# A gated-mixer layer on one core: half of the convolution's input tiles by seven products in place of eight, and 20 host tiles for 36 attention units

## The chip, the cores and the metric

The kernel runs on one core of a Trainium2 chip. The metric is the device time of one execution in microseconds (us); the median of the runs shown is used. Engines are named as in the profile: PE (TensorE's matmuls), PEld (its weight loads), DVE (VectorE), ACT (ScalarE), POOL (GpSimd), SP (SyncE, which issues most DMAs).

## The reference

One layer of a streaming encoder for 1024 prompt frames and 32 sample frames, width 1024, in float32:

```python
h = rms_norm(x, g_mix)
z = h @ w_in                       # [q | k | v | conv_h | conv_B | conv_C | gate_a | gate_b]
a = window_attn(q, k, v) @ w_attn_out          # 16 heads, 4 kv heads, band of 2 to 3 chunks of 64
u = cc * ch
conv = u[t-2] * conv_w[0] + u[t-1] * conv_w[1] + u[t] * conv_w[2]
bo = (cb * conv) @ w_conv_out
x = x + (sigmoid(ga) * a + sigmoid(gb) * bo) @ w_mix_out
x = x + memory_cross_attention(rms_norm(x)) ; x = x + relu(rms_norm(x) @ w_up)**2 @ w_down
```

The last two rows of `u` of each request group are an output too (`o_conv`).

## The kernel before

**Arithmetic.** Each float32 operand is split into a rounded part and a rest, and a product is three matmuls. Tokens lie in three chunks c of 384, 384 and 288 columns. A weight tile is 1024 rows by 128 columns, held as 128x1024; `gemm` (L195) runs it over one chunk in 24 matmuls. `fetch_w` (L147) loads a tile by SP, `issue_w` (L164) splits it on ACT (L129) and DVE (L130), two tiles ahead of use, in the order of the list `worder`.

**Stages** in the order of the program, one weight tile after another:

1. Norms, the first query tiles and the memory's keys and values, to about 85 us.
2. The attention stage, to about 547 us. 32 *hosts*, each one weight tile over three chunks: the 24 convolution tiles C, H and B of the eight f, six query tiles, one key tile and one gate tile. 36 attention units (4 kv heads times 8 blocks and a sample block) are strung between the hosts' chunks, each as `scores`, `turn` (transposes) and `values`: about one unit per host. Between scores and turn lies a softmax on DVE, ACT and POOL. `do_conv` (L633) puts the scaling of t for C and B on POOL (L649, L664, L666) and stores B's result to `bc_d`.
3. A gate tile, three `gate_a2` and eight `do_attn_out` (L831), to about 657 us. In these the operands of the seven-product form are made (`gx_steps`).
4. Seven `gate_pair` (L936): the tiles of gate_a and gate_b of one f, over chunks 0 and 1, by seven half products (`product`, L887, 12 matmuls) in place of eight, in the Strassen-Winograd form: each needs two sums of the pair's weights (`g_sum`) and sums of the activations (b11, b21, t2, n1, n3, b22, n4). Chunk 2 goes by `gate_c2`, an ordinary gemm. To about 775 us.
5. `do_conv_out` (L1072), for each chunk eight tiles: bc times w_conv_out, times the gate, plus the attention's part `m1_d`, added on POOL for f = 0 to 6 (L1081) and on DVE for f = 7. Then `do_mix` (L1087), which needs all eight results of its chunk. Then cross-attention and the MLP, whose matrices also go partly by weight sums.

**Weight sums on POOL.** `sum_step` (L729) makes them in *pieces*: a load by POOL's own DMA queue (L739 or L741) into one of two tiles (`ws` and `xacc`, by turns), four adds of 128x256 (L746), a store to HBM (L750 or L752). A piece of kind "g" is half a gate pair's sum of w_in, "u" one of w_up, and the other 32 are of w_down. One call starts the load of the next piece and finishes the piece before it. The pieces are a list, 14 g, then 32 of w_down, then 4 u; `sum_step` is called at 29 places in the hosts, then in stages 3 and 4. All its instructions are pinned, that is they keep their order on POOL. A tile's next load waits until its store has landed.

**What sets the order.** The program is written as a list of items; a scheduler with a model of the machine then fixes the order of the instructions on each engine, except of those that are pinned. Each engine runs its list strictly in order, so POOL's other operations wait behind a piece that waits.

Of the kernel before, what the change touches and what calls it, by code (L numbers as in the profile page):

```python
# [40 lines left out]
def hybrid_step(ctx: ExitStack, tc: tile.TileContext, io):  # L41
# [492 lines left out]
    def do_KS(kv):  # L534
# [18 lines left out]
        ksp[kv] = (hi, lo, ch, cl, b, bs)

    class Unit:
# [5 lines left out]
        def scores(self):  # L561
            kv, p = self.kv, self.p
            hi, lo, ch, cl, bias, bs = ksp[kv]
            if self.sample:
                G, nk = 1, 256
# [34 lines left out]
            for h in range(G):  # L600
                dve.tensor_scalar_mul(stl[:, h, :nk], stl[:, h, :nk], rec[:, h : h + 1])
# [31 lines left out]
    def do_conv(which, f, extras=()):  # L633
        def fn(w):
# [84 lines left out]
    pieces = [("g", f, q) for f in PAIRS for q in range(2)]  # L719
# [9 lines left out]
    def sum_step():  # L729
        old = W.pop("new", None)  # L730
        if pieces:
            at = pieces.pop(0)
            t = sum_tile(len(pieces))
            if at[0] in ("g", "u"):
                kind, f, q = at
                for e in range(2):
                    src = io["w_in"][34 + 8 * e + f] if kind == "g" else io["w_up"][UP[f][e]]
# [5 lines left out]
        if old:  # L743
# [3 lines left out]
            if at[0] in ("g", "u"):  # L747
                kind, f, q = at
                for w in range(2):
                    pin(pool_e.dma_start((gsum_d[f - 1] if kind == "g" else usum_d[f])[:, w, :, 256 * q : 256 * q + 256], t[:, 2 * w : 2 * w + 2]))  # L750
# [184 lines left out]

    def gate_pair(f):  # L936
        def take(key):
            k, w = ready.pop(0)
            assert k == key, (k, key)
            return w  # L940
# [26 lines left out]
        if f == 1:  # L967
            pump(4)
# [1092 lines left out]
```

## Time and profile before

| | us |
|---|---|
| median of 3 runs | 1737.74 (1737.34 to 1739.08) |
| profiled execution, device time | 1739.95 |
| its span | 1738.2 |
| TensorE busy | 1722.8 |
| POOL busy | 600.7 |
| last attention store issued on POOL | 549.50 |
| last weight-sum store issued on POOL | 773.73 |
| end of the first mix tile, on DVE | 839.43 |

A timeline row gives start, duration, engine, line, operation, output<-input, and in brackets the idle time before it and what ended it. A row of a group gives the number of instructions, their busy time and mean, and after the bar the engine's idle time ahead of them with its releasers. A row of windows gives a stretch, its length, the busy time of PE, PEld, DVE, ACT and POOL, the granted clock, the DMA engines' busy share and the rate in GB/s.

### The profile page before, as it was taken

Reading aid. Unit: us, or ns where it says so; the run is one execution under the profiler, and the core shown is the slowest. Engines: PE = TensorE matmul, PEld = TensorE weight load, DVE = VectorE, ACT = ScalarE, POOL = GpSimd, SP = SyncE. Lnnn points to the kernel's source line nnn. Section 1 sums busy time; section 2 is a strip of 40 time slices with the busy share of each in tenths; the row PEclk is TensorE's granted clock in tenths of the full one; section 3 lists DMA queues with packets and bytes.
Section 4 is the critical chain, followed back from the end, with each engine's and each line's share of the span. In section 5 each row is a group of like instructions: output and inputs, shape, how many; then the busy total and the mean of one; then the engine's idle time right before and its main releaser. Section 6 shows DMA issues by size and latency. Waiting matters only on the chain.

```text
span 1738.2 us, 32563 instructions
## 1 busy us (share of the span) xinstructions
PE 1722.8 (99%) x12238; PEld 1707.1 (98%) x12238; DVE 1194.9 (69%) x2276; ACT 854.0 (49%) x1666; POOL 600.7 (35%) x671
## 2 busy tenths in 40 slices
PE   9999999999999999999999999999999999999998
PEld 8999999999999999999999999999999999999998
DVE  7776776867766656555677888687666686546675
ACT  8653533535335324434556666765444553333444
POOL 0026366453643444552225242106555410000122
PEclk9999999999999999999999999999999999999999
DMA  5343344333445888867766667676666695554555
GB/s 186 98 131 121 125 134 137 131 131 133 150 141 193 291 302 282 294 221 233 272 222 200 216 229 253 226 266 201 221 220 220 215 316 186 187 196 164 199 165 168
DMA packets 179853, 346.60 MB, mean 199 GB/s; under 512 B 18656, under 2 KB 101248, under 8 KB 179568
## 3 DMA queue, kind: packets, MB, share of 16 engines
q1 hardware_dynamic: 163504, 290.07, 50.5%
q0 software_dynamic: 15568, 53.68, 8.9%
q8 instruction: 96, 1.57, 0.4%
q10 hardware_dynamic: 624, 0.77, 0.1%
q14 instruction: 61, 0.50, 0.1%
HBM read 250.73 MB, written 93.14 MB: 198 GB/s over the span
## 4 chain that ended last, share of the span: by engine, by line
PE 93%; DMA 3%; DVE 2%; ACT 1%; issue 1%; POOL 0%; SPq 0%; DVEq 0%; ACTq 0%; POOLq 0%
PE acc L200 13%; PE acc L202 13%; PE acc L201 13%; PE acc L892 6%; PE acc L893 6%; PE acc L894 6%; PE acc L1832 6%; PE acc L1834 6%; PE acc L1833 6%; PE pc L892 2%; PE pc L894 2%; PE pc L893 2%; PE pt L609 2%; PE sc L584 1%; PE sc L583 1%; PE pa L201 1%
## 5 line engine op out<-in xcount | busy, mean ns | idle before, releaser
L129 ACT CAST wh<-wr 128x1024 fp32r<-128x1024 f32 (+1 forms) x214 | 223.8, 1046 | 361.9 <-PE acc L1833 124.8
L130 DVE TENSOR_TENSOR wl<-wr,wh 128x1024 fp32r<-128x1024 f32 (+1 forms) x214 | 276.6, 1293 | 109.7 <-ACT wh L129 108.4
L200 PE MATMUL acc<-X,wh 128*128 128x384 f32 (+1 forms) x864 | 281.4, 326 | 0.0
L201 PE MATMUL acc<-X,wh 128*128 128x384 f32 (+1 forms) x864 | 278.9, 323 | 0.0
L202 PE MATMUL acc<-X,wl 128*128 128x384 f32 (+1 forms) x864 | 277.8, 322 | 0.0
L287 POOL TENSOR_TENSOR xacc<-xacc,ct 128x384 f32<-128x384 f32 (+1 forms) x55 | 74.8, 1364 | 364.0 <-ACT ct L285 362.3
L201 PEld LDWEIGHTS acc<-X,wh 128*128 128x128 f32 x864 | 162.7, 188 | 1.6 <-DVE X L291 0.7
L200 PEld LDWEIGHTS acc<-X,wh 128*128 128x128 f32 x864 | 162.4, 188 | 0.8
L202 PEld LDWEIGHTS acc<-X,wl 128*128 128x128 f32 x864 | 162.4, 188 | 0.1
L200 PE MATMUL acc<-Y,wh 128*128 128x384 f32 (+1 forms) x432 | 139.8, 324 | 2.2 <-DVE ct L1080 2.2
L202 PE MATMUL acc<-Y,wl 128*128 128x384 f32 (+1 forms) x432 | 139.3, 323 | 1.3 <-DMA wl<-wl_d 1.3
L201 PE MATMUL acc<-Y,wh 128*128 128x384 f32 (+1 forms) x432 | 139.5, 323 | 0.0
L129 ACT CAST PTh<-pt 128x512 fp32r<-128x512 f32 (+3 forms) x94 | 45.9, 517 | 112.2 <-PE pt L609 110.5
L1834 PE MATMUL acc<-n,wl 128*128 128x264 f32 x352 | 100.0, 285 | 0.8 <-DVE wl L130 0.8
L1832 PE MATMUL acc<-n,wh 128*128 128x264 f32 x352 | 100.3, 285 | 0.2 <-ACT wh L129 0.2
L1833 PE MATMUL acc<-n,wh 128*128 128x264 f32 x352 | 100.1, 284 | 0.0
L746 POOL TENSOR_TENSOR ws<-ws 128x256 f32<-128x256 f32 x100 | 96.2, 962 | 5.8 <-DMA ws<-in_w_up 0.2
L746 POOL TENSOR_TENSOR xacc<-xacc 128x256 f32<-128x256 f32 x100 | 85.4, 854 | 5.7 <-DMA xacc<-in_w_in 0.4
L200 PEld LDWEIGHTS acc<-Y,wh 128*128 128x128 f32 x432 | 81.1, 188 | 3.1 <-DVE ct L1080 3.1
L202 PEld LDWEIGHTS acc<-Y,wl 128*128 128x128 f32 x432 | 81.1, 188 | 1.6 <-DMA wl<-wl_d 1.6
L201 PEld LDWEIGHTS acc<-Y,wh 128*128 128x128 f32 x432 | 81.1, 188 | 0.5 <-DVE Y L803 0.5
L595 ACT ACTIVATE S<-S,nmx 128x257 f32<-128x257 f32 (+1 forms) x132 | 64.2, 488 | 19.9 <-DVE nmx L590 18.6
(446 smaller groups left out, 5562.2 us busy)
## 6 DMA issues: line engine op xcount, KB each, us to landing
wr<-in_w_up SPq DMA_DIRECT2D x53, 512.0 KB, 4.4
wr<-in_w_in SPq DMA_DIRECT2D x52, 512.0 KB, 3.6
wr<-wsum_d SPq DMA_DIRECT2D x40, 512.0 KB, 3.5
wr<-in_w_conv_out SPq DMA_DIRECT2D x24, 512.0 KB, 4.0
wr<-in_w_mix SPq DMA_DIRECT2D x24, 512.0 KB, 4.5
wr<-in_w_down SPq DMA_DIRECT2D x24, 512.0 KB, 3.6
n_d<-Z SPq DMA_DIRECT2D x32, 264.0 KB, 4.3
xacc<-in_w_down POOLq DMA_DIRECT2D x16, 512.0 KB, 4.8
```

The costliest lines, as they stand in the source:

```text
L129: act.copy(hi, src)
L130: dve.tensor_sub(lo, src, hi.bitcast(F32))
L200: pe.matmul(out, wh[:, a], hi, start=(k == 0), stop=False)
L201: pe.matmul(out, wh[:, a], lo, start=False, stop=False)
L202: pe.matmul(out, wl[:, a], hi, start=False, stop=(k == len(acts) - 1))
L746: pin(pool_e.tensor_tensor(t[:, to], t[:, x], t[:, y], op=ALU.add))
L892: pe.matmul(acc, wh[:, a], hi, start=(start and k == 0), stop=False, skip_group_check=True)
L893: pe.matmul(acc, wh[:, a], lo, start=False, stop=False, skip_group_check=True)
L894: pe.matmul(acc, wl[:, a], hi, start=False, stop=(k == 3), skip_group_check=True)
L1832: pe.matmul(a, wh[:, s], hi, start=(t == 0 and k == 0), stop=False, skip_group_check=True)
L1833: pe.matmul(a, wh[:, s], lo, start=False, stop=False, skip_group_check=True)
L1834: pe.matmul(a, wl[:, s], hi, start=False, stop=(t == 1 and k == 7), skip_group_check=True)
```

## The change

Four things are changed together.

- **Twelve convolution tiles go by seven products.** The C, H and B tiles of f = 4 to 7 leave the hosts and become six `conv_pair` (C, H, B of f = 4 and 5, then of 6 and 7), each in the form of a gate pair, ahead of the seven gate pairs. Their sums add 12 pieces of kind "g", at the front of the list; `gsum_d` grows from 7 to 13 pairs.
- **20 hosts for 36 units.** A table `begin` gives the third of a host (a chunk) in which each unit's scores begin, its turn comes two thirds later and its values three. `sum_step` is called in 18 hosts.
- Half of the heads' scaling by the reciprocal goes from DVE to ACT (`act.mul`), and the loads of the cached keys come in a step of their own (`do_KC`).
- In the gate pairs u2 and v lie in tiles that exist anyway (`tmp`, `g22`); the third weight tile of the pairs (`third`) and the loads of the operands (`pump(4)`) begin at the first conv pair; `o_conv` is stored in two halves.

```diff
+    HBC = {"H": 0, "B": 1, "C": 2}
+    CPAIRS = [(which, f) for f in (4, 6) for which in "CHB"]
+    ptiles = [(10 + 8 * HBC[which] + f, 11 + 8 * HBC[which] + f) for which, f in CPAIRS]
+    ptiles += [(34 + f, 42 + f) for f in PAIRS]
-    pieces = [("g", f, q) for f in PAIRS for q in range(2)]
+    pieces = [("g", i, q) for i in range(len(ptiles)) for q in range(2)]
     pieces += [(j, t, i) for j in range(4) for t in range(2) for i in range(4)]
     pieces += [("u", i, q) for i in range(2) for q in range(2)]
...
-                dve.tensor_scalar_mul(stl[:, h, :nk], stl[:, h, :nk], rec[:, h : h + 1])
+                if h < G // 2:
+                    act.mul(stl[:, h, :nk], stl[:, h, :nk], rec[:, h : h + 1])
+                else:
+                    dve.tensor_scalar_mul(stl[:, h, :nk], stl[:, h, :nk], rec[:, h : h + 1])
...
-    conv = [(which, f) for f in range(NF) for which in "CHB"]
+    conv = [(which, f) for f in range(4) for which in "CHB"]
-    hosts += take(6) + [("Q", 1, 0), ("Q", 1, 1)]
-    hosts += [("K", 1)] + take(5) + [("Q", 2, 0), ("Q", 2, 1)]
-    hosts += take(6) + [("Q", 3, 0), ("Q", 3, 1)]
-    hosts += take(7) + [("G", 0)]
+    hosts += take(3) + [("Q", 1, 0), ("Q", 1, 1)]
+    hosts += [("K", 1)] + take(2) + [("Q", 2, 0), ("Q", 2, 1)]
+    hosts += take(3) + [("Q", 3, 0), ("Q", 3, 1)]
+    hosts += take(4) + [("G", 0)]
+    begin = [[1, 2, 3, 5, 6, 8, 10, 11, 13]] + [[0, 1, 3, 5, 6, 8, 10, 11, 13]] * 2 + [[0, 1, 3, 4, 6, 7, 9, 10, 12]]
...
+            slots[at][3].append(u.scores)
+            slots[at + 2][1].append(u.turn)
+            slots[at + 3][0].append(u.values)
...
-        if i % 2 and i > 1 or i > 3:
+        if i > 1:
             extras.append((1, sum_step))
...
+    def conv_C(f, c, x, s):
+        n = CH[c][1]
+        t = ct2[f, c] = slot(ga_pool, f"Ga{c}", n, F32)
+        if c == 2:
+            dve.tensor_mul(t, x, R[2])
+            pool_e.tensor_tensor(t, t, R[2], op=ALU.mult)
+        elif s is None:
+            act.copy(t, x)
+        else:
+            dve.tensor_sub(t, x, s)
+    def conv_H(f, c, x, s):
...
+            pool_e.tensor_copy(u[:, 258:260], prm[:, STATE0 + 2 * f : STATE0 + 2 * f + 2])
...
+        u = cu[f, c] = slot(G["pool"], f"Gb{c}", n, F32)
+        if s is None:
+            dve.tensor_mul(u, x, t)
+        else:
+            dve.tensor_sub(u, x, s)
+            pool_e.tensor_tensor(u, u, t, op=ALU.mult)
+    def conv_edges(f):
+        pool_e.tensor_copy(cu[f, 2][:, 0:2], cu[f, 1][:, 382:384])
...
+    def conv_B(f, c, x, s):
...
+        if c == 2:
+            act.mul(b, u[:, :m], taps[0])
...
+        else:
+            act.mul(b, u, taps[2])
...
+        if c == 2:
+            pool_e.tensor_tensor(t[:, :npr], b[:, :npr], R[c][:, :npr], op=ALU.mult)
+            pool_e.tensor_tensor(t[:, npr:], b[:, npr + 2 :], R[c][:, npr:], op=ALU.mult)
+            dve.tensor_mul(t, x, t)
+        elif s is None:
+            dve.tensor_mul(t, x, t)
+        else:
+            dve.tensor_sub(t, x, s)
+            pool_e.tensor_tensor(t, t, b, op=ALU.mult)
+        sp.dma_start(bc_d[c][:, f], t)
+    def conv_pair(i):
...
+        product(A1, w1, 0, op("b11"), True)
+        s1 = Y["top"].tile([P, 384], F32, tag="s1", name=nm("s1"))
+        act.copy(s1, A1)
...
+        product(A1, w1, 1, op("b21"), False)
+        out(f, 0, A1, None)
+        pump(0)
+        out(f, 2, gate_c2(w1), None)
...
+        product(B, w4, 0, op("t2"), True)
...
+        sum_step()
...
+        out(f + 1, 1, B, v)
+        sum_step()
...
+        if which == "H":
+            conv_edges(f)
+            conv_edges(f + 1)
...
+    for i, (t1, t2) in enumerate(ptiles):
+        worder.extend([("w_in", t1), ("g_sum", i, 0), ("g_sum", i, 1), ("w_in", t2)])
+        if i < len(CPAIRS):
+            item(lambda i=i: conv_pair(i))
+        else:
+            item(lambda f=PAIRS[i - len(CPAIRS)]: gate_pair(f))
```

In the changed program L757 are the adds of a piece, L750 and L752 its loads, L761 and L763 its stores; L962 is POOL's product in `conv_C`, L982 that in `conv_H`, L985 to L987 the copies in `conv_edges`, L998 and L1002 ACT's `act.mul` in `conv_B`, L1010, L1011 and L1017 POOL's products there, L1034 the copy of s1, L1209 POOL's add of the conv output.

POOL's order before, from the last pieces to the first adds of the conv output (usum_d and in_w_up belong to kind "u", ct to the conv output):

```order
L750 DMA usum_d<-ws_7671 128x2x256 x2
L739 DMA ws_7775<-in_w_up 128x2x256 x2
L746 TENSOR_TENSOR xacc_7728<-xacc_7728 128x256 x4
L750 DMA usum_d<-xacc_7728 128x2x256 x2
L746 TENSOR_TENSOR ws_7775<-ws_7775 128x256 x4
L750 DMA usum_d<-ws_7775 128x2x256 x2
L1081 TENSOR_TENSOR ct_9363<-ct_9363,ct_9336 128x384
L1081 TENSOR_TENSOR ct_9415<-ct_9415,ct_9388 128x384
L1081 TENSOR_TENSOR ct_9467<-ct_9467,ct_9440 128x384
```

POOL's order after, at the first adds of the conv output (wsum_d is a piece of w_down):

```order
L757 TENSOR_TENSOR xacc_8204<-xacc_8204 128x256 x4
L763 DMA wsum_d<-xacc_8204 128x1024
L1209 TENSOR_TENSOR ct_9499<-ct_9499,ct_9472 128x384
L750 DMA xacc_8354<-in_w_up 128x2x256 x2
L757 TENSOR_TENSOR ws_8248<-ws_8248 128x256 x2
L1209 TENSOR_TENSOR ct_9551<-ct_9551,ct_9524 128x384
L757 TENSOR_TENSOR ws_8248<-ws_8248 128x256 x2
L763 DMA wsum_d<-ws_8248 128x1024
L1209 TENSOR_TENSOR ct_9603<-ct_9603,ct_9576 128x384
L750 DMA ws_8400<-in_w_up 128x2x256 x2
```

Before, all pieces stood ahead of the first add; now the last piece of w_down and the u pieces stand between the first adds of chunk 0.

POOL's order after, in the first H pair (Gb and Ga are u and t of `conv_H`, u_... the third chunk's u; nothing stands here in before):

```order
L752 DMA xacc_6290<-in_w_down 128x1024
L757 TENSOR_TENSOR ws_6250<-ws_6250 128x256
L982 TENSOR_TENSOR Gb_1282_7119<-Gb_1282_7119,Ga_1254_6923 128x384
L757 TENSOR_TENSOR ws_6250<-ws_6250 128x256
L985 COPY u_7196<-Gb_1282_7119 128x2
L982 TENSOR_TENSOR Gb_1284_7141<-Gb_1284_7141,Ga_1256_6944 128x384
L757 TENSOR_TENSOR ws_6250<-ws_6250 128x256
L985 COPY u_7062<-Gb_1284_7141 128x2
L757 TENSOR_TENSOR ws_6250<-ws_6250 128x256
```

The products of u and the two-column copies into the third chunk's u stand between the adds of a w_down piece, behind its load.

ACT's order after, at the first B pair (wh is a weight tile's split, s_ the copy s1):

```order
L1002 ACTIVATE ct_7241<-Gb_1273_7035,prm 128x384
L129 CAST wh_7144<-wr_1278_7070 128x1024
L129 CAST wh_7165<-wr_7148 128x1024
L998 ACTIVATE ct_7272<-u_7062,prm 128x290
L129 CAST wh_7223<-wr_7169 128x1024
L1002 ACTIVATE ct_7334<-Gb_1282_7119,prm 128x384
L1034 COPY s_1297_7221<-acc_7206 128x384
L129 CAST wh_7281<-wr_1300_7227 128x1024
```

The reads of u_7062 and Gb_1282, which POOL writes, stand ahead of the copy of s1 and of a weight's split.

More of the change, by code (lines that the diff above doesn't have):

```diff
@@ L736, in sum_step @@
                 for e in range(2):
-                    src = io["w_in"][34 + 8 * e + f] if kind == "g" else io["w_up"][UP[f][e]]
+                    src = io["w_in"][ptiles[f][e]] if kind == "g" else io["w_up"][UP[f][e]]
                     src = src.rearrange("p (h c) -> p h c", h=2)
@@ new lines, in conv_pair @@
+    def conv_pair(i):
+        which, f = CPAIRS[i]
+        t1, t2 = ptiles[i]
+        out = {"C": conv_C, "H": conv_H, "B": conv_B}[which]
+        op = lambda kind: [gop[kind, k] for k in range(4)]
+        w1 = take_w(("w_in", t1))
+        if i == 0:
+            cvt.append(Y["top"].tile([P, 4, 4], F32, name="cvt2"))
+            third.update(n=2, pool=Y["top"])
+            fetch_w()
+            pump(4)
+        A1, B, C = (acc_tile([P, 384]) for _ in range(3))
+        product(A1, w1, 0, op("b11"), True)
+        s1 = Y["top"].tile([P, 384], F32, tag="s1", name=nm("s1"))
+        act.copy(s1, A1)
+        issue_w()
+        fetch_w()
+        product(A1, w1, 1, op("b21"), False)
+        out(f, 0, A1, None)
+        pump(0)
+        out(f, 2, gate_c2(w1), None)
+        issue_w()
+        fetch_w()
+        w4 = take_w(("g_sum", i, 0))
+        product(B, w4, 0, op("t2"), True)
+        u2 = slot(G["pool"], "Gb0", 384, F32)
+        dve.tensor_sub(u2, B, s1)
+        sum_step()
+        w3 = take_w(("g_sum", i, 1))
+        product(C, w3, 1, op("n1"), True)
+        v = slot(G["pool"], "Gb1", 384, F32)
+        dve.tensor_add(v, C, s1)
+        product(B, w3, 0, op("n3"), False)
+        out(f + 1, 1, B, v)
+        sum_step()
+        product(C, w4, 1, op("b22"), False)
+        out(f, 1, C, u2)
+        issue_w()
+        fetch_w()
+        w2 = take_w(("w_in", t2))
+        product(B, w2, 1, op("n4"), False)
+        out(f + 1, 0, B, s1)
+        issue_w()
+        fetch_w()
+        out(f + 1, 2, gate_c2(w2), None)
+        if which == "H":
+            conv_edges(f)
+            conv_edges(f + 1)
+        if which == "H" and f + 1 == NF - 1:
+            sp.dma_start(io["o_conv"][:, 4:], cvt[0])
@@ L985, in gate_pair @@
         fetch_w()
-        w4 = take(("g_sum", f - 1, 0))
+        w4 = take(("g_sum", len(CPAIRS) + f - 1, 0))
         product(B, w4, 0, op("t2"), True)
         load_a(1)
-        u2 = Y["top"].tile([P, 384], F32, tag="u2", name=nm("u2"))
-        dve.tensor_sub(u2, B, s1)
+        t = tmp(384)
+        dve.tensor_sub(t, B, s1)
         sum_step()
@@ L993, in gate_pair @@
             pump(1)
-        w3 = take(("g_sum", f - 1, 1))
+        w3 = take(("g_sum", len(CPAIRS) + f - 1, 1))
         product(C, w3, 1, op("n1"), True)
-        v = Y["top"].tile([P, 384], F32, tag="v", name=nm("v"))
-        dve.tensor_add(v, C, s1)
+        g22 = gate_slot(1, f)
+        dve.tensor_add(g22, C, s1)
         product(B, w3, 0, op("n3"), False)
-        g22 = gate_slot(1, f)
-        dve.tensor_sub(g22, B, v)
+        dve.tensor_sub(g22, B, g22)
         sg[1][f] = into(g22, g22)
```

98 lines of the change are left out of this document (58 added, 40 removed).

## The prediction

> **What bounds the kernel now.** I read the page's summary first, then the windows by stage, then the POOL timeline, because TensorE looks full and the change hands POOL more work. The page:
>
> ```profile
> span 1738.2 us, 32563 instructions
> ...
> PE 1722.8 (99%) x12238; PEld 1707.1 (98%) x12238; DVE 1194.9 (69%) x2276; ACT 854.0 (49%) x1666; POOL 600.7 (35%) x671
> ...
> PE 93%; DMA 3%; DVE 2%; ACT 1%; issue 1%; POOL 0%; SPq 0%; DVEq 0%; ACTq 0%; POOLq 0%
> ```
>
> PE holds 99% of the span and 93% of the chain that ended last; POOL is 35% busy and on no link of that chain. The windows, one row each for the attention stage, the attention output projection, the gate pairs and the start of the conv output (columns: span; busy us of PE, weight load, DVE, ACT, POOL; clock; DMA share; GB/s):
>
> ```profile
> 100.00:545.00 445.00, 445.00 (x2875) 438.15 (x2874) 317.68 (x795) 194.86 (x475) 214.54 (x316) 1.00 0.39 129
> 545.00:657.00 112.00, 111.96 (x712) 111.54 (x711) 67.06 (x97) 39.14 (x78) 52.62 (x67) 1.00 0.89 297
> 657.00:775.00 118.00, 118.00 (x731) 118.00 (x730) 74.72 (x99) 51.03 (x84) 63.88 (x75) 1.00 0.82 271
> 775.00:800.00 25.00, 25.00 (x156) 25.00 (x154) 10.58 (x16) 7.12 (x11) 1.18 (x2) 1.00 0.59 194
> ```
>
> PE waits nowhere in these 700 us, at a granted clock of 1.00, so fewer matmuls are worth their full time as long as nothing else becomes late. POOL's "busy" (52.62 of 112) misleads: it leaves out waiting and DMA issue. Its timeline in the same stretch:
>
> ```profile
> 549.50 0.70 POOL L631 DMA_DIRECT2D ao_d<-AO  x1 [4.04 <-DVE AO L628]
> ...
> 550.65 3.73 POOL L746 TENSOR_TENSOR xacc<-xacc 128x256 f32<-128x256 f32 x4
> 554.79 0.56 POOL L752 DMA_DIRECT2D wsum_d<-xacc  x1 [0.41 <-POOL xacc L746]
> 559.74 0.54 POOL L741 DMA_DIRECT2D xacc<-in_w_down  x1 [4.38 <-DMA wsum_d<-xacc]
> 560.29 5.57 POOL L746 TENSOR_TENSOR ws<-ws 128x256 f32<-128x256 f32 x4
> ...
> 632.80 0.54 POOL L741 DMA_DIRECT2D ws<-in_w_down  x1 [4.81 <-DMA wsum_d<-ws]
> 633.35 3.80 POOL L746 TENSOR_TENSOR xacc<-xacc 128x256 f32<-128x256 f32 x4
> 637.56 0.59 POOL L752 DMA_DIRECT2D wsum_d<-xacc  x1 [0.41 <-POOL xacc L746]
> 642.97 0.54 POOL L741 DMA_DIRECT2D xacc<-in_w_down  x1 [4.83 <-DMA wsum_d<-xacc]
> ...
> 727.19 4.43 POOL L746 TENSOR_TENSOR ws<-ws 128x256 f32<-128x256 f32 x4
> ...
> 737.55 4.28 POOL L746 TENSOR_TENSOR xacc<-xacc 128x256 f32<-128x256 f32 x4
> ...
> 750.38 5.12 POOL L746 TENSOR_TENSOR ws<-ws 128x256 f32<-128x256 f32 x4
> ...
> 763.12 3.19 POOL L746 TENSOR_TENSOR xacc<-xacc 128x256 f32<-128x256 f32 x4
> ...
> 773.73 1.45 POOL L750 DMA_DIRECT2D usum_d<-ws  x2 [0.41 <-POOL ws L746]
> 798.81 1.00 POOL L1081 TENSOR_TENSOR ct<-ct,ct 128x384 f32<-128x384 f32 x1 [23.63 <-DMA mkr<-mk_d]
> ```
>
> Each weight-sum piece is a serial round on POOL: adds, store, wait until that store has landed (4.4 to 4.8 us), load into the freed tile, adds of the other tile. From 550.65 to 727.19 there are 17 rounds: 10.38 us each for a w_down piece ("w"). A w_up piece ("u", two issues per load and store, as the "g" pieces of w_in have) takes 12.83 and 12.74. So POOL is already saturated there, and finishes at 773.73, some 25 us before its next task at 798.81. That is all the slack it has.
>
> **The change part by part.** *Matmuls.* Six pairs save one of eight half products each, 12 matmuls of 128x384, so 72. One takes 0.174 us: 24 run from 370.42 to 374.61.
>
> ```profile
> 370.42 0.34 PE L200 MATMUL acc<-X,wh 128*128 128x384 f32 x1
> ...
> 374.61 0.33 PE L200 MATMUL acc<-X,wh 128*128 128x384 f32 x1
> ```
>
> 72 x 0.174 = 12.5 us, all on the path, since PE is full before and after.
>
> *The attention stage.* Twelve hosts leave it. A host is two chunks of 24 matmuls at 4.19 and one of 288 columns at 4.19 x 288/384 = 3.14: 11.52 us; twelve are 138 us. The last attention store (549.50) comes at about 411, the first adds behind it at about 412. The 36 units now sit on 20 hosts. DVE's cover: it was busy 317.68 of 445.
>
> ```profile
> L130 DVE TENSOR_TENSOR wl<-wr,wh 128x1024 fp32r<-128x1024 f32 x32 | 43.9, 1370 | 12.1 <-ACT wh L129 12.1
> L601 DVE TENSOR_SCALAR S<-S,rec 128x256 f32<-128x256 f32 (+1 forms) x129 | 43.0, 393 | 1.2
> L662 DVE SCALAR_TENSOR_TENSOR ct<-u,prm,ct 128x384 f32<-128x384 f32 (+1 forms) x48 | 34.8, 729 | 3.9 <-ACT ct L660 3.4
> L667 DVE TENSOR_TENSOR ct<-acc,ct 128x384 f32<-128x384 f32 (+1 forms) x24 | 12.5, 520 | 23.9 <-issue 15.0 <-PE acc L202 3.7 <-PE pt L609 2.9
> L653 DVE TENSOR_TENSOR u<-acc,Ga 128x384 f32<-128x384 f32 (+1 forms) x24 | 12.3, 511 | 17.2 <-PE pt L609 11.4 <-PE acc L202 5.8
> L648 DVE TENSOR_TENSOR Ga<-acc,R 128x384 f32<-128x384 f32 (+1 forms) x22 | 11.4, 519 | 29.8 <-PE acc L202 29.7
> ```
>
> Half of the conv rows (71.0/2 = 35.5), twelve weight splits (16.4) and half of the L601 scaling, which goes to ACT (21.5), leave: 244 of 307 us, 80%, against 71%. Tighter, but not full, and PE's own matmuls still cover the softmax chain; I cost it at 0 and keep a bound of 0.5 us per unit, 18 us, as a rival. ACT gains the 21.5 us on a load of 44%: 0. Reusing tmp and g22 for u2 and v, two QC buffers, the split store of o_conv and do_KC issued later hang on nothing late: 0.
>
> *POOL.* Pieces grow from 50 to 62, and steps in hosts fall from 29 to 18. After the last attention store stood 21 w and u pieces; now, by the order, 43 stand before the seventh add of the conv output (9 g, 32 w, 2 u), and mix needs that add. The time that they have grows only by the six conv pairs: seven half products of 12 matmuls at 0.174 and two gemms of 3.14, 20.9 us each, 125 in all. In the first 112 us after attention DMA is as loaded as at 0.89 before, so g is taken at 12.5, by the u rounds. In the attention and gate stages (19 w) a w takes 10.4. The conv pairs have no row. At a DMA share of 0.39 a round took
>
> ```profile
> 462.15 0.54 POOL L741 DMA_DIRECT2D ws<-in_w_down  x1 [3.55 <-DMA wsum_d<-ws]
> ...
> 470.75 0.60 POOL L741 DMA_DIRECT2D xacc<-in_w_down  x1 [0.87 <-DMA wsum_d<-xacc]
> ```
>
> 8.60 us from load to load, with some 1.2 us of other POOL operations in it; so 7.4 and 10.4 are the ends. Conv pairs move two weight tiles, two sums and about one and a half pieces in and out per 20 us, with fewer spills than the gate stage: I put them near a share of 0.7 and take 9.3 for 13 w. The 2 u: 12 each. Sum: 9 x 12.5 + 19 x 10.4 + 13 x 9.3 + 2 x 12 = 455 us.
>
> POOL also gets operations of the conv pairs. Those that the order puts between load and store (the rest hide behind a store's landing) are priced by
>
> ```profile
> L664 POOL TENSOR_TENSOR ct<-ct,R 128x384 f32<-128x384 f32 x16 | 16.6, 1040 | 24.2 <-DVE ct L662 24.1
> L649 POOL TENSOR_TENSOR Ga<-Ga,R 128x288 f32<-128x288 f32 x8 | 7.4, 922 | 6.4 <-DVE Ga L648 6.4
> L664 POOL TENSOR_TENSOR ct<-ct,R 128x256 f32<-128x256 f32 x8 | 6.0, 750 | 6.1 <-DVE rec L599 6.1
> L666 POOL TENSOR_TENSOR ct<-ct,R 128x32 f32<-128x32 f32 x8 | 3.3, 408 | 0.0
> L1081 POOL TENSOR_TENSOR ct<-ct,ct 128x384 f32<-128x384 f32 x14 | 22.6, 1611 | 70.2 <-DVE ct L1080 33.2 <-DMA mkr<-mk_d 23.6 <-DMA ct<-m_d 9.1
> ```
>
> 9 x 1.04 + 3 x 0.92 + 1 x (0.75 + 0.41) + 4 x 1.61 and some 2 us of small copies: 22 us. The last piece's landing and load, 6 us, lie behind the add. The seventh add ends at 412 + 455 + 22 - 6 = 883, its split at 884. When would PE want it?
>
> ```profile
> 839.43 0.56 DVE L1095 TENSOR_TENSOR Ga<-acc,ct 128x384 f32<-128x384 f32 x1 [0.50 <-DMA ct<-in_x]
> ```
>
> That is the end of the first mix tile, so its start is 839.43 - 4.19 = 835.2, less 12.5: 822.7. PE waits 884 - 822.7 = 61 us. Part of this shows earlier: in a B pair ACT waits at L998 for POOL's u (L982, L985) with the copy of s1 (L1034) queued behind it, and PE can't go on in that accumulator. The order puts u of the first B pair behind 9 g and 5.5 w rounds: 412 + 112 + 53 = 577; PE wants it at 409 + 112 + 42 + 2 = 565. 12 us; the second B pair by the same count some 10 us more.
>
> A row against a rule: a 512 KB store of POOL is waited for 4.4 to 4.8 us here, from 0.56 us after its issue began. The Trainium skill, DMA: Bandwidth & Descriptors, section "Anatomy of one DMA — SWDGE (gpsimd) path", gives for such a DMA 2.0 us plus the bytes over 436 GB/s, an estimate of 3.2 us; the trace comes near it only where DMA share is low (3.55), and by the rule alone the sum would lose over 1.5 us per round.
>
> Net: -12.5 + 61 = +48.5. The profiled execution took 1739.95 us for its span of 1738.2, 2.2 above the median of 1737.74: 1788.5 for a profile, 1786 for the median.
>
> **Ends.** High: w at 10.4 in the conv pairs too (+14.3), g and u at 12.8 (+4): 1805. Low: rounds at 7.4 in all stages, which end POOL's list before 822: no wait at all, 1725.2. A mean w of 8.4 against my 9.95 is the point where the change is worth nothing (49 us over 32 pieces).
>
> **The rivals.** (1) *POOL keeps up; PE alone sets the time.* If a store lands in about 3.2 us under load as well, w rounds take 3.75 + 0.41 + 0.56 + 3.2 + 0.54 = 8.4, g rounds some 2 us less, and POOL's list ends near 814, ahead of 822.7: 1737.74 - 12.5 = 1725.2, faster. For it: 3.55 at a share of 0.39. Against: 17 rounds in a row at 10.38 in just such stages. It is also what the skill's page would make of it. Chance 0.10. (2) *Only the B pairs wait.* The two waits for u cost 22 us, PE's lateness lets POOL catch up, and by mix nothing is left: 1725.2 + 22 = 1747. It needs w near 9.0 in the gate stage; against it 10.38. Chance 0.12. (3) *The attention stage is the bound*: 1.8 units per host, with DVE at 80% and each unit's turn waiting 0.5 us for its softmax, and POOL in time: 1725.2 + 18 = 1743, slower. For it: DVE's margin shrinks from 29% to 20%; against: a mean is not a queue, and POOL must keep up as well. Chance 0.05. (1) is also the case in which the change does what it says. The forecast has 0.73.
>
> **How the numbers follow.** A measurement of this kernel tells 0.2%, 3.5 us, from no change. Faster is rival 1: 0.10. Rivals 2 and 3 and the forecast are slower, less 0.04 for mixtures of small waits that come out within 0.2%: 0.86. The range takes the forecast's high end, 1806, and reaches down over rival 2 to 1744, leaving out rivals 1 and 3.
>
> **What would show it.** Right: in the profile after, PE's busy share falls to about 96%; POOL's rounds at L752, L757 and L763 follow without a gap from about 412 to past 860; PE idles at two B pairs, released over ACT's L998 by POOL, and a longer time ahead of mix, with POOL L1209 as the last link. Wrong: PE full through the gate pairs, w rounds under 8.4 us, POOL idle ahead of conv output; or gaps of PE inside the 20 hosts with DVE as releaser.

## The result and the profile after

| kernel | median us | runs | ratio to before (95% interval) |
|---|---|---|---|
| before | 1738.41 | 4 | |
| changed | 1764.49 (1761.61 to 1768.13) | 4 | 1.0151 (1.0126 to 1.0177) |

The changed kernel is 26 us slower; 48 were forecast, in a range that holds the measured time. Its profiled execution took 1761.61 us. The page of the changed kernel:

```profile
span 1759.8 us, 32539 instructions
...
PE 1720.3 (98%) x12166; PEld 1699.7 (97%) x12166; DVE 1218.1 (69%) x2242; ACT 894.6 (51%) x1748; POOL 665.4 (38%) x763
...
PE 77%; DMA 9%; POOL 8%; DVE 3%; issue 3%; ACT 1%; SPq 0%; ACTq 0%; POOLq 0%; DVEq 0%
```

POOL and DMA, which here means mostly the landings of POOL's stores (wsum_d leads its lines), are now 17% of the chain that ended last, where they had 3%. PE's row hides part of the loss: 72 matmuls fewer should have taken 12.5 us off its busy time, and only 2.5 are off, mostly because part of its work ran at a lower clock. The windows by stage (attention, attention output, conv pairs, gate pairs, conv output):

```profile
100.00:411.00 311.00, 311.00 (x2036) 304.19 (x2036) 248.44 (x659) 201.54 (x517) 143.46 (x214) 1.00 0.40 126
411.00:525.00 114.00, 112.14 (x716) 111.53 (x715) 68.85 (x98) 40.38 (x79) 63.88 (x82) 1.00 0.83 281
525.00:655.00 130.00, 124.76 (x767) 124.29 (x767) 84.80 (x111) 37.04 (x51) 81.97 (x113) 0.99 0.63 213
655.00:790.00 135.00, 132.45 (x817) 131.58 (x816) 74.13 (x97) 48.44 (x77) 70.57 (x87) 1.00 0.80 274
790.00:870.00 80.00, 65.67 (x337) 62.34 (x336) 44.46 (x57) 28.01 (x46) 49.00 (x59) 0.89 0.77 262
```

The attention stage is as full as before (311.00 of 311). TensorE is idle in the conv pairs (5.2 us), a little in the gate pairs (2.6), and above all at the start of the conv output (14.3), where its clock is 0.89 as well. Summed over windows of 0.5 us from 100 to 960, idle time (length less PE's busy time) is 26.0 us and lost clock (busy time times one less the granted clock) 6.9; in the kernel before 1.3 and 0. The windows have to be short: a window's clock is its mean over idle time too, and with windows of 20 us the lost clock would come out as 8.1. So -12.5 + 24.7 + 6.9 = +19.1 of the 21.6 us between the two spans; 2.5 us are not accounted for.

What holds TensorE at the conv output, on POOL, ACT, DVE and PE in order of time:

```profile
816.31 0.59 POOL L763 DMA_DIRECT2D wsum_d<-xacc  x1 [0.41 <-POOL xacc L757]
816.92 1.00 POOL L1209 TENSOR_TENSOR ct<-ct,ct 128x384 f32<-128x384 f32 x1
...
817.95 0.51 ACT L129 CAST M<-ct 128x384 fp32r<-128x384 f32 x1 [14.12 <-POOL ct L1209]
...
818.50 0.56 DVE L130 TENSOR_TENSOR M<-ct,M 128x384 fp32r<-128x384 f32 x1 [13.41 <-ACT M L129]
818.97 1.02 DVE L837 TENSOR_TENSOR Y<-ct,Y 128x384 fp32r<-128x384 f32 x2
...
819.91 0.55 DVE L1208 TENSOR_TENSOR ct<-acc,Ga 128x384 f32<-128x384 f32 x1
...
820.61 0.66 PE L200 MATMUL acc<-Y,wh 128*128 128x384 f32 x1 [8.57 <-DVE ct L1208]
```

One add waits on POOL for a piece that is stored at 816.31. ACT's split of that add's result waits for it (14.12 us), DVE's half of the split waits for ACT's, and DVE's reading of a finished accumulator (L1208) stands behind that. So TensorE waits for an accumulator, two engines away from POOL. SP stood behind the same add: its next load for the conv output (L1204) waited 15.2 us for it, with weight loads behind.

```profile
SPq L1204 <- POOL ct L1209: 22.8, 6, 15.2
```

POOL's list itself (stores of the first two and the ninth g piece behind attention, of the last w_down piece, and the seventh add):

```profile
406.61 0.69 POOL L638 DMA_DIRECT2D ao_d<-AO  x1
...
418.54 1.47 POOL L761 DMA_DIRECT2D gsum_d<-ws  x2 [0.41 <-POOL ws L757]
431.26 1.47 POOL L761 DMA_DIRECT2D gsum_d<-xacc  x2 [0.41 <-POOL xacc L757]
...
506.49 1.48 POOL L761 DMA_DIRECT2D gsum_d<-ws  x2 [0.42 <-POOL ws L757]
...
826.79 0.57 POOL L763 DMA_DIRECT2D wsum_d<-ws  x1 [0.41 <-POOL ws L757]
...
853.85 1.02 POOL L1209 TENSOR_TENSOR ct<-ct,ct 128x384 f32<-128x384 f32 x1
```

Eight g rounds in 87.95 us are 11.0 each (12.5 were taken), 32 w rounds in 320.3 us are 10.0 with POOL's operations for the conv pairs in them (10.4 were taken with these). The seventh add ends at 854.9, not 883.

The wait at the first B pair took another way than forecast. SP's queue, then ACT, POOL, DVE and PE:

```profile
571.47 0.80 SPq L1018 DMA_DIRECT2D bc_d<-ct  x2
573.06 0.32 SPq L159 DMA_DIRECT2D wr<-gsum_d  x1
586.43 0.32 SPq L1018 DMA_DIRECT2D bc_d<-ct  x1
586.86 0.37 SPq L159 DMA_DIRECT2D wr<-in_w_in  x1
588.02 0.32 SPq L1018 DMA_DIRECT2D bc_d<-ct  x1
588.44 0.58 SPq L159 DMA_DIRECT2D wr<-in_w_in  x1
...
592.44 1.05 ACT L129 CAST wh<-wr 128x1024 fp32r<-128x1024 f32 x1 [5.09 <-DMA wr<-in_w_in]
...
592.56 0.60 POOL L752 DMA_DIRECT2D ws<-in_w_down  x1 [4.57 <-DMA wsum_d<-ws]
...
596.22 0.23 POOL L1011 TENSOR_TENSOR ct<-ct,R 128x32 f32<-128x32 f32 x1
...
596.48 0.46 DVE L1012 TENSOR_TENSOR ct<-pa,ct 128x288 f32<-128x288 f32 x1 [6.04 <-POOL ct L1011]
596.86 2.92 DVE L130 TENSOR_TENSOR wl<-wr,wh 128x1024 fp32r<-128x1024 f32 x1
...
599.82 0.50 PE L202 MATMUL pa<-X,wl 128*128 128x288 f32 x1 [4.71 <-DVE wl L130]
```

SP issues nothing for 13 us: its next entry is the store of a B result whose product (L1017) stands on POOL behind a piece, and the weight loads stand behind that store. So ACT's half of a weight's split comes late and ends at 593.49. But that isn't what ended last: DVE's half (L130) stands in DVE's queue behind L1012, which waited 6.04 us for another product of POOL's (L1011), and this one stood behind the landing of a store and part of the next piece. TensorE ran out of work at 595.11 (599.82 - 4.71). In this pair DVE's half takes 1.21 to 2.94 us, so right behind ACT's half it would have ended between 594.7 and 596.4: by this estimate SP's delay alone would have cost 1.3 us at most. SP's waits in 500 to 900 us:

```profile
SPq L1018 <- POOL ct L1017: 28.2, 6, 13.0
```

### The profile page after: what moved, and what is told of

The parts are those of the page before. It is cut to its first block, busy times and chain, and to the rows that moved or that the text cites. A ratio compares the mean times of both kernels' runs of the same rounds, so it can differ in the third digit from the quotient of the medians.

```text
span 1759.8 us, 32539 instructions
## 1 busy us (share of the span) xinstructions
PE 1720.3 (98%) x12166; PEld 1699.7 (97%) x12166; DVE 1218.1 (69%) x2242; ACT 894.6 (51%) x1748; POOL 665.4 (38%) x763
## 4 chain that ended last, share of the span: by engine, by line
PE 77%; DMA 9%; POOL 8%; DVE 3%; issue 3%; ACT 1%; SPq 0%; ACTq 0%; POOLq 0%; DVEq 0%
PE acc L200 9%; PE acc L202 9%; PE acc L201 9%; PE acc L1960 6%; PE acc L1962 6%; PE acc L1961 6%; PE acc L906 5%; PE acc L907 5%; PE acc L908 5%; DMA wsum_d<-ws 4%; POOL xacc L757 3%; DMA wsum_d<-xacc 3%; POOL ws L757 3%; PE pc L906 2%; PE pc L908 2%
## 5 line engine op out<-in xcount | busy, mean ns | idle before, releaser
L129 ACT CAST wh<-wr 128x1024 fp32r<-128x1024 f32 (+1 forms) x226 | 236.3, 1047 | 419.3 <-PE acc L1961 119.0
L130 DVE TENSOR_TENSOR wl<-wr,wh 128x1024 fp32r<-128x1024 f32 (+1 forms) x226 | 297.3, 1316 | 113.9 <-ACT wh L129 112.5
L200 PE MATMUL acc<-X,wh 128*128 128x384 f32 (+1 forms) x576 | 188.0, 326 | 0.0
L201 PE MATMUL acc<-X,wh 128*128 128x384 f32 (+1 forms) x576 | 186.8, 324 | 0.0
L202 PE MATMUL acc<-X,wl 128*128 128x384 f32 (+1 forms) x576 | 185.8, 323 | 0.0
L200 PE MATMUL acc<-Y,wh 128*128 128x384 f32 (+1 forms) x432 | 142.2, 330 | 16.3 <-DVE ct L1208 14.1
L201 PE MATMUL acc<-Y,wh 128*128 128x384 f32 (+1 forms) x432 | 141.2, 327 | 0.1
L757 POOL TENSOR_TENSOR ws<-ws 128x256 f32<-128x256 f32 x124 | 109.7, 885 | 6.9
L757 POOL TENSOR_TENSOR xacc<-xacc 128x256 f32<-128x256 f32 x124 | 107.0, 863 | 6.8
L201 PEld LDWEIGHTS acc<-X,wh 128*128 128x128 f32 x576 | 108.5, 188 | 1.0
L200 PEld LDWEIGHTS acc<-X,wh 128*128 128x128 f32 x576 | 108.3, 188 | 0.8
L202 PEld LDWEIGHTS acc<-X,wl 128*128 128x128 f32 x576 | 108.3, 188 | 0.7
L200 PEld LDWEIGHTS acc<-Y,wh 128*128 128x128 f32 x432 | 82.5, 191 | 18.7 <-ACT wh L129 8.9
L906 PE MATMUL acc<-Y,wh 128*128 128x264 f32 (+1 forms) x232 | 72.1, 312 | 3.6 <-DVE ct L1117 1.1
```

Of the source, the lines that this page charges most:

```text
L129: act.copy(hi, src)
L130: dve.tensor_sub(lo, src, hi.bitcast(F32))
L200: pe.matmul(out, wh[:, a], hi, start=(k == 0), stop=False)
L201: pe.matmul(out, wh[:, a], lo, start=False, stop=False)
L202: pe.matmul(out, wl[:, a], hi, start=False, stop=(k == len(acts) - 1))
L757: pin(pool_e.tensor_tensor(t[:, to], t[:, x], t[:, y], op=ALU.add))
```

## The experiments

Twelve kernels. The theory is that of the prediction: POOL's pieces of weight sums, each a serial round, are late, and what stands behind them in POOL's queue holds the others. Rivals are named in each expectation. "Idle" and "lost clock" are the sums over windows of 0.5 us as above, in the one execution of each kernel that was profiled.

| label | median us | ratio to before (95%) | idle, lost clock us |
|---|---|---|---|
| e1_30_steps | 1759.08 | 1.0138 (1.0101 to 1.0175) | 22.3, 7.4 |
| e2_adds_dve | 1769.09 | 1.0191 (1.0156 to 1.0226) | 27.5, 8.7 |
| e3_before_18 | 1775.89 | 1.0220 (1.0200 to 1.0241) | 36.3, 4.4 |
| e4_b_dve | 1768.48 | 1.0180 (1.0160 to 1.0199) | 31.9, 7.9 |
| e7_two_by_two | 1759.74 | 1.0141 (1.0090 to 1.0192) | 24.8, 5.0 |
| e8_conv_dve | 1774.46 | 1.0196 (1.0176 to 1.0215) | 41.9, 6.1 |
| e10_two_conv_dve | 1757.14 | 1.0109 (1.0091 to 1.0127) | 14.4, 3.9 |
| e11_two_24_conv_dve | 1746.25 | 1.0043 (1.0026 to 1.0060) | 16.1, 6.7 |
| f1_two_24_all_dve | 1737.21 | 1.0000 (0.9988 to 1.0011) | 8.0, 3.1 |
| f2_two_18_all_dve | 1755.89 | 1.0095 (1.0073 to 1.0117) | 21.0, 2.8 |
| f4_one_24_all_dve | 1735.95 | 0.9983 (0.9970 to 0.9996) | 8.1, 1.7 |
| f5_f1_scale_dve | 1742.62 | 1.0019 (1.0004 to 1.0033) | 11.2, 1.7 |

**The kernel before with the changed kernel's number of steps** (no conv pairs at all):

```diff
-        if i % 2 and i > 1 or i > 3:
+        if i > 13:
             extras.append((1, sum_step))
```

> The kernel before with sum steps in 18 hosts in place of 29; no conv pairs, nothing else changed. Theory (POOL's backlog): 11 more rounds of about 10 us follow attention, the order puts 29 pieces of w_down and one of w_up ahead of the seventh add, 551 + 29 x 10.0 + 12.8 + some 10 us of adds = 864 us against 835 wanted, so 29 us of idle TensorE and some 8 us of lowered clock: 1738 + 30 to 37 = 1768 to 1775 us. Rival A (conv pairs' own operations): 1738 us, no change.

1775.89 us, one us above what was expected, with none of the conv pairs' code. Its windows at the gate pairs' end and behind it:

```profile
775.00:800.00 25.00, 25.00 (x155) 25.00 (x154) 12.75 (x15) 6.66 (x11) 12.77 (x14) 1.00 0.72 251
800.00:840.00 40.00, 13.68 (x65) 12.85 (x64) 9.95 (x11) 5.63 (x9) 22.10 (x30) 0.66 0.55 186
```

TensorE is full to 800 and then idle for 26 of 40 us at a clock of 0.66. ACT's waits there name the same chain as in the changed kernel:

```profile
ACT M L129 <- POOL ct L1081: 45.6, 7, 33.8
```

The backlog of pieces is enough for a loss larger than the whole change shows. Rival A gave 1738 for this kernel; what the conv pairs' own operations cost in the changed kernel is tested further down.

**30 steps in the hosts of the changed kernel:**

```diff
         if i > 1:
             extras.append((1, sum_step))
+        if i > 1 and i % 3 != 2:
+            extras.append((2, sum_step))
```

> The changed kernel with 30 sum steps in the hosts in place of 18 (a second one in 12 of them), so that 12 more pieces are done inside the attention stage. Theory (POOL's backlog of pieces): all pieces end near 412 + 32 x 10.0 + 4 x 12.8 = 783 us, ahead of the first add of the conv output; the 13 us of idle TensorE and the 8 us of lowered clock there go, 1764.5 - 21 = 1743 us; if the first B pair's wait goes too, 7 us less, 1736; down to 1727 if everything was the backlog. Rival A (the conv pairs' own operations and the loads behind them cost it, wherever the pieces stand): 1757 to 1765 us. Rival B (POOL has no room in the attention stage: pieces there delay the softmax): the time stays above 1755 us and TensorE idles between 100 and 411.

1759.08 us: a miss by 16, and by the number alone it is rival A's, though the step it was made for came true. TensorE has no idle at the conv output any more (less than 0.3 us in each window of 20 us from 780 to 880). It lost the gain elsewhere: 5.3 us of idle and 1.7 of clock inside the attention stage (rival B in part), 4.4 with the clock at 440 to 460, 4.2 at 540 to 560, and at the first B pair 9.6, by the very chain of the prediction: ACT waited 10.6 us for POOL's u, and PE 7.15 us for the copy of s1 behind it. So more steps in the hosts cure the end of the list, not the pairs.

**The conv output's adds on DVE:**

```diff
-            (dve if f == NF - 1 else pool_e).tensor_tensor(t, t, t1, op=ALU.add)
+            dve.tensor_tensor(t, t, t1, op=ALU.add)
```

> The changed kernel with the conv output's add on DVE for all f, POOL's pieces unchanged. Theory (the adds wait in POOL's queue behind pieces, ACT's copy waits for the add and everything else on ACT waits behind that copy): idle TensorE between 805 and 860 us goes from 13 us to about 2, its clock there is 1.00 again, 1764.5 - 20 = 1744 us. Rival A (conv pairs' own operations): 1757 to 1765 us, since this stage isn't theirs. Rival C (the conv output waits for loads at a DMA share of 0.9): 1760 us or more.

1769.09 us, a miss. The idle time moved on by some 50 us. ACT, then PE:

```profile
873.46 0.52 ACT L285 ACTIVATE xacc<-Ga 128x384 f32<-128x384 f32 x1 [11.22 <-DMA usum_d<-xacc]
...
875.58 0.69 PE L200 MATMUL acc<-M,wh 128*128 128x384 f32 x1 [8.57 <-ACT wh L129]
```

The pieces' second tile, xacc, is also the accumulator of the squares in mix. With the adds out of the way, ACT waits for the last store from that tile, and a weight's split for ACT. The list has two takers at its end, and moving one of them leaves the other: the list itself must end earlier. DMA load (rival C) wasn't it, since 800 to 840 runs with 1.4 us of idle.

**The B pairs' product on DVE:**

```diff
-            pool_e.tensor_tensor(t, t, b, op=ALU.mult)
+            dve.tensor_tensor(t, t, b, op=ALU.mult)
         sp.dma_start(bc_d[c][:, f], t)
```

> The changed kernel with the last product of the B pairs (three of 128x384 in each pair) on DVE in place of POOL. Theory: SP's store of the B result no longer waits for POOL with weight loads behind it, so the 4.7 us of idle TensorE at the first B pair and the 1.7 us of lowered clock behind it go, the conv output's waits stay or shrink by the 6 us of POOL time freed: 1752 to 1759 us. If the wait were ACT's on POOL's u (as predicted), it would stay: 1764 us.

1768.48 us, a miss. The weight loads come in time now (no wait of ACT's splits there is for a load), and yet the wait is there, by the same last link, on DVE and then PE:

```profile
599.03 0.46 DVE L1012 TENSOR_TENSOR ct<-pa,ct 128x288 f32<-128x288 f32 x1 [6.13 <-POOL ct L1011]
...
601.01 0.51 PE L202 MATMUL pa<-X,wl 128*128 128x288 f32 x1 [2.86 <-DVE wl L130]
```

So the edit took away SP's wait, but what held TensorE was DVE behind POOL's product L1011, which stayed on POOL. The loss at the B pairs shrinks from 6.4 us with the clock to 4.6, but at the conv output (800 to 860) idle and lost clock grow from 19 us to 26: the scheduler now sets all w_down pieces ahead of the first add, where the changed kernel has 31 of 32, and ACT waits 22.5 us for the first. An edit far from the queue's end moves the end.

**Pieces two by two**, the first of three ways to make POOL faster: both adds and stores, then both loads, at every second call.

```diff
     def sum_step():
-        old = W.pop("new", None)
...
+        W["calls"] = W.get("calls", 0) + 1
+        if W["calls"] % 2:
+            return
+        for at, t in W.pop("new", []):
...
+        for _ in range(2 if pieces else 0):
```

> The changed kernel with POOL's pieces taken two by two: adds and store of the one, adds and store of the other, then both loads, so that a store's landing lies beside the other piece's adds. All 62 pieces stay, in the same number. By the measured parts two pieces take 2 x (3.75 + 0.57) + a rest of the landings of some 5 + 2 x 0.55 = 15 us in place of 20. Theory (the wait for a store's landing in each round makes POOL late): about 7.5 us per piece, all pieces end near 412 + 11 x 9 + 36 x 7.7 + 20 = 800 us at the latest, ahead of the conv output's adds; idle TensorE and lowered clock between 800 and 860 us go (20 us), 1764.5 - 20 = 1744 us, with the B pairs' waits left or smaller: 1735 to 1748 us. Rival D (the rate of POOL's transfers beside the weight loads is the limit, not the serial round): a piece still takes over 9.5 us, and the time stays at 1760 us or more.

1759.74 us, a miss by 12: rounds are shorter (two w pieces take 17.2 us on average, 13.9 to 21.1, so rival D's 9.5 us per piece is out), the idle at the conv output is 1.6 us, so the theory's half holds; but the B pairs got worse, and this is the chain as the prediction had it, on ACT and then PE:

```profile
578.90 0.54 ACT L999 ACTIVATE ct<-u,prm 128x290 f32<-128x290 f32 x1 [13.11 <-POOL u L986]
579.35 0.46 ACT L1035 COPY s<-acc 128x384 f32<-128x384 f32 x1
```

```profile
579.86 0.69 PE L907 MATMUL acc<-X,wh 128*128 128x384 f32 x1 [9.70 <-ACT s L1035]
```

A pair of pieces blocks POOL twice as long, and u's copy stands behind it.

**The conv pairs' POOL operations on DVE**, with pieces one by one, two by two, and with 24 steps. The products of `conv_C`, `conv_H` and `conv_B`, and the copies into u:

```diff
-            pool_e.tensor_tensor(u, u, t, op=ALU.mult)
+            dve.tensor_tensor(u, u, t, op=ALU.mult)
...
-        pool_e.tensor_copy(cu[f, 2][:, 0:2], cu[f, 1][:, 382:384])
+        dve.tensor_copy(cu[f, 2][:, 0:2], cu[f, 1][:, 382:384])
```

(and the others likewise; the 24 steps add `if i > 1 and i % 3 == 0: extras.append((2, sum_step))`). The two copies into `cvt` were left on POOL, though the expectations say that every operation moved.

> The changed kernel with every POOL operation of the conv pairs (products, copies of the edges) on DVE; the pieces unchanged. Theory: no instruction of the conv pairs waits behind a piece, so the 5 us of idle TensorE and 1.6 us of lowered clock there go; the conv output's adds still stand behind pieces and their 13 us idle and 7 us of clock stay, by the order they are even 1 or 2 rounds later: 1755 to 1770 us. Rival A (the conv pairs' own chain, on whichever engine): idle TensorE between 560 and 660 us stays at 5 us or more.

1774.46 us, above the expected range by 4. The conv pairs ran without idle time until 640, so it isn't their own chain (rival A); 800 to 880 lost 38 us with the clock, as all of w_down and a u piece came ahead of the adds (ACT waited 31.4 us for the first).

> Both of the last two: pieces two by two, and the conv pairs' POOL operations on DVE. Theory: neither the conv pairs nor the conv output wait for a piece, TensorE is idle for some 5 us between 100 and 900: 1738.5 - 12.5 + 5 = 1727 to 1735 us, ahead of the kernel before. Rival A or D: 1745 us or more.

1757.14 us, a miss by 22. The profiled execution took 1748.19, 9 us less than the median, so what the other executions lost beyond it no trace shows. In it the conv output is nearly free (3.3 us with the clock), and one large wait is left, on SP:

```profile
SPq L1070 <- POOL cvt L988: 26.0, 1, 26.0
```

That is the second half of the `o_conv` store. It waits for POOL's copy into cvt, which stands behind pieces, and the weight loads of the first gate pair stand behind it on SP; PE waited 9.6 us. Nobody reads `o_conv` in the kernel. The kernel before this one, e8_conv_dve, has the same wait, 19.6 us on SP and 3.6 on PE.

> The same with 24 sum steps in the hosts (calls work on two pieces at every second one, so 24 pieces). Theory: 6 pieces more are done before the conv pairs; since the backlog is gone already, nothing more to gain: within 4 us of the kernel with 18. If the attention stage has no room on POOL for them, 3 to 8 us slower, with idle TensorE between 200 and 411 us as in the kernel with 30 steps.

1746.25 us, 11 us better and not "within 4": by the medians the steps were still worth something. The two profiled executions (1748.19 and 1750.60) don't show where.

**The copies into cvt on DVE too:**

```diff
-        pool_e.tensor_copy(cvt[0][:, f - 4, 0:2], cu[f, 2][:, 256:258])
+        dve.tensor_copy(cvt[0][:, f - 4, 0:2], cu[f, 2][:, 256:258])
```

> The changed kernel with 24 sum steps in the hosts, pieces two by two, and every POOL operation of the conv pairs on DVE, the two copies into cvt included, which the three kernels before this one had left on POOL. Theory: there SP waited 26 us with its store of o_conv for POOL's copy into cvt, with weight loads behind it; without POOL in the conv pairs that wait goes, and with it the 7 to 10 us of idle TensorE and 3 to 4 us of lowered clock at the first gate pair: 1746 - 10 = 1736 us, down to 1728 if the idle at 520 to 550 us goes too. Rival E (the first gate pair waits for its weight sums in gsum_d or for a full DMA system): 1744 us or more, with ACT's split still waiting for gsum_d over 5 us.

1737.21 us in 11 runs, 9 less than with the copies on POOL, and the kernel before's time. Idle time at the first gate pair is gone (0.7 us).

> The same with the 18 sum steps of the changed kernel in the hosts. Theory (SP's wait for POOL's copy into cvt cost the kernel with 18 steps its time): 1757 less some 14 us of idle and clock at the first gate pair, 1740 to 1745 us, and within 5 us of the one with 24. Rival E: 1755 us.

1755.89 us, rival E's number. But the idle at the first gate pair went as the theory said (at most 0.7 us in each 20 us from 640 to 720), and no split of ACT's waited for gsum_d there, so rival E is out; nor is it within 5 us of the one with 24, since with TensorE on time there, the conv output waited for POOL's list again. POOL at the list's end with 18 steps:

```profile
814.45 1.46 POOL L750 DMA_DIRECT2D usum_d<-ws  x2 [0.41 <-POOL ws L746]
815.93 1.00 POOL L1210 TENSOR_TENSOR ct<-ct,ct 128x384 f32<-128x384 f32 x1
```

PE waited 12.5 us for that add, in the same way as before. Six pieces more in the hosts are worth 18.7 us here: a dose of the backlog, with nothing else changed in the program.

**24 steps, nothing of the conv pairs on POOL, pieces one by one:**

> The kernel with 24 sum steps and no POOL operation of the conv pairs, but with the pieces one by one again. Theory (serial rounds of 10 us against some 8.5 two by two): the 37 pieces behind attention end near 412 + 3 x 11.3 + 32 x 9.9 + 2 x 12.8 = 788 us for the first adds and 805 us for the last, 45 us later than two by two, so the conv output waits again for 5 to 15 us with lowered clock behind it: 1743 to 1757 us. Rival F (two by two only makes DMA bursts; the steps and DVE did it all): 1737 us or less.

1735.95 us in 10 runs, a miss: rival F's number, and the only kernel ahead of the one before, by 0.2% (0.9983). Two by two does shorten a round, to 8.2 us from 9.7 in these two kernels, so the first half of rival F's reason is wrong; the second half stands, since the steps and DVE are enough here. The list's end, one by one with 24 steps:

```profile
789.72 1.46 POOL L761 DMA_DIRECT2D usum_d<-ws  x2 [0.41 <-POOL ws L757]
795.55 1.00 POOL L1211 TENSOR_TENSOR ct<-ct,ct 128x384 f32<-128x384 f32 x1 [4.37 <-DVE ct L1210]
```

Now POOL waits for the add, 4.4 us. The list ended some 14 us earlier than the expectation had it for its last piece, in time, but with less than half a round to spare.

**All scaling back on DVE** in the kernel of 1737.21 us:

```diff
-                if h < G // 2:
+                if h < 0:
                     act.mul(stl[:, h, :nk], stl[:, h, :nk], rec[:, h : h + 1])
```

> The kernel that equals the one before (24 sum steps, two by two, no POOL operation in the conv pairs), with all heads' scaling back on DVE as in the kernel before, in 20 hosts. If ACT's share of the scaling is needed for 36 units in 20 hosts (DVE's share there rises from about 80 to 87%), TensorE idles between 100 and 411 us and the time rises by 5 to 18 us, 1742 to 1755 us. If DVE's margin was never the limit, as predicted: within 3 us of 1737 us.

1742.62 us, 5 more; the two come from two chips, and their intervals to before overlap (1.0004 to 1.0033 and 0.9988 to 1.0011), so the loss is likely but not clear. The attention stage without and with ACT's half of the scaling:

```profile
100.00:411.00 311.00, 307.28 (x2000) 297.99 (x1999) 272.52 (x722) 171.91 (x449) 167.42 (x244) 1.00 0.43 136
```

```profile
100.00:411.00 311.00, 309.93 (x2023) 302.31 (x2024) 249.49 (x660) 200.52 (x515) 170.83 (x249) 1.00 0.44 138
```

DVE goes to 88% and TensorE's idle from 1.1 to 3.7 us, in pieces of under 1 us that wait for DVE and for the softmax. That is 2.6 of the 5 us; the rest isn't in this stage. So 36 units fit 20 hosts almost without cost at 80% of DVE, and seem to begin to cost at 88%.

## Why the prediction was right, and by how much it was not

*Matmuls, -12.5 us.* Right. In the fastest variant idle and lost clock sum to 9.8 us against 1.3 before; -12.5 + 6.8 + 1.7 = -4.0, and its span of 1735.4 is 2.8 below 1738.2. The saving is there, to within 1.2 us, and is what the waits eat.

*The attention stage, 0.* Right: 311.00 of 311 busy, DVE at 80% (244 of 307 were worked out, 248 of 311 measured). ACT's 201.5 us, 65%, cost nothing. Rival 3 is out for the changed kernel.

*POOL is late, 61 us.* Right in kind: the backlog alone makes the kernel before 37 us slower, and with six pieces more in the hosts the conv output's wait goes. The size is the step that was off: rounds. 9 g at 11.0 in place of 12.5, and the w rounds at 10.0 with the conv pairs' operations in them in place of 10.4, took 12 or 13 us each off the sum; the few us left are not taken apart. The seventh add came at 854.9 instead of 883, which leaves 33 us of wait by the prediction's own subtraction (855.9 - 822.7), against 24.7 idle and 6.9 of lost clock in the windows. The g price of 12.5 had been borrowed from the u rounds, and no row of the kernel before had a g round under such load.

*Where TensorE waits.* Half right. It was to wait ahead of mix; it waited at the conv output's own tiles, from the first add on, because ACT's split and DVE's eviction stand behind that add. The two B pairs were to cost 22 us, by ACT's wait for u with the copy of s1 behind it; they cost 6.9 with the clock, by DVE's wait for POOL's product L1011 with a weight's split behind it. The engine that is late was right, the queue that passes it on was not. The predicted chain was seen whole in the kernels with 30 steps and two by two, so it is a mechanism of this program, but in the changed kernel ACT waited for u only 8.4 us in two waits, covered. Of the signs that were named, PE's busy share did not fall to 96%: it is 98%, as the loss was half the size and part of it is lowered clock, which counts as busy.

*The split store of o_conv, 0.* Wrong: it was said to hang on nothing late. In the changed kernel SP waited 5.5 us for it, under cover; with pieces two by two and the pairs' other operations on DVE it was 26 us and cost 9.6 of TensorE. A store that nobody reads holds a queue that everybody needs.

*Lowered clock.* Not in the sum. Of TensorE's loss about a fifth is this (6.9 of 31.6 us): after its wait of 4.71 us at the first B pair, the clock in the next windows of 2 us of the changed kernel was

```profile
600.00:602.00 2.00, 2.00 (x9) 2.00 (x10) 0.70 (x2) 0.00 (x0) 0.00 (x0) 0.50 0.92 264
602.00:604.00 2.00, 2.00 (x10) 2.00 (x9) 0.00 (x0) 0.00 (x0) 0.90 (x2) 0.65 0.67 260
604.00:606.00 2.00, 2.00 (x14) 2.00 (x13) 0.56 (x1) 1.06 (x1) 1.84 (x3) 1.00 0.79 219
```

half, then rising to full within 4 us: 9 and 10 matmuls in a window in place of 14. The Trainium skill, TensorE: Matmul & The Clock Gate, section "Part 1: The HAM clock gate (the "warmup" mystery)", states that an idle window of about 3.4 us brings the array down to half its clock, and a busy one of that length brings it back; these rows agree, with 4.71 us of idle time and a full clock again within 4 us.

*The rivals.* Rival 1 (1725) is out: w rounds took 10.0 us, and the median landing of a POOL store of 512 KB in the conv and gate pairs was 3.6 to 4.8 us. The estimate of 3.2 us by the fit in the Trainium skill, DMA: Bandwidth & Descriptors, section "Anatomy of one DMA — SWDGE (gpsimd) path", is below all of these. *Rival 2* had the B pairs alone; they are the smaller part. The range was wide enough to hold its 1747 too, so that the measured time lies inside says less than the account by parts.

What stays open: how much of the conv output's lost clock would go with the idle alone, since no kernel has one without the other; and whether a third tile for the pieces would do what two by two does, which no run here shows.

## What to carry to other kernels

An engine that is off the chain and 35% busy can be the next bound: count its rounds from start to start, waits included, and ask when its list ends, before handing it more work and less time. Work with no deadline (sums for a later stage, a store that nobody reads) must not stand in a queue ahead of work that has one; look along every in-order queue that the changed step touches, SP's too. Waits of TensorE from 2.2 to 25 us cost 1.4 to 3.1 us more in clock here, nearly always, and the long ones no more than the short ones, so several small waits are worse than they look.

## What the runs showed of the hardware

- A single idle time of 2.6 us, shorter than the window of about 3.4 us that the Trainium skill states (same page and section as above), was enough for the clock to fall; the measurement decides. In the fastest kernel, TensorE waited 2.62 us up to 440.51, and the next windows were

```profile
440.00:442.00 2.00, 1.43 (x7) 1.02 (x7) 1.51 (x3) 1.54 (x4) 1.84 (x3) 0.83 0.73 259
442.00:444.00 2.00, 2.00 (x7) 2.00 (x8) 1.15 (x2) 0.00 (x0) 1.58 (x3) 0.50 0.02 6
```

  In the kernel with the adds on DVE, a wait of 2.16 us (up to 672.50) was followed by a clock of 0.50 too, and one of 2.38 us (up to 441.20) was not, so the length alone doesn't tell.

- What a fall costs hardly depends on the length of the wait: 1.7 us of lost clock behind waits of 2.16, 2.62 and 4.71 us, 2.1 behind 9.6 (the kernel with two by two and the conv pairs on DVE) and 2.4 behind 25.4 (the kernel before with 18 steps).

- A chain of waits can stay the same in kind and change engines: with the same backlog, TensorE was held by way of ACT and DVE (the changed kernel's conv output), of DVE behind a product of POOL's (the first B pair), of ACT's copy (pieces two by two), of SP's store of `o_conv` (two by two with the pairs' products on DVE), or of a shared tile (adds on DVE).
